# A recurrence chain among projections: updates by heads, halves of the copies swapped, and an ordering clock with other lags

## The chip, the core and the metric

The kernel runs on one core of a Trainium2 chip. The core's engines work side by side, each through its own queue in order: TensorE (PE in the profile, its weight loads PEld), VectorE (DVE), ScalarE (ACT), GpSimd (POOL) and SyncE (SP), which here starts transfers. They meet only at semaphores. The metric is the time of one launch in microseconds (us) on the device; several runs are taken, and their median counts.

## The reference

One inference step of a decoder layer in float32, for a prompt of 1024 positions and for 8 sequences of 4 new positions (the sample), with a width of 1024:

```
z = x @ w_in                       # 62 column tiles of 128 for each part of the input
RWKV-7 branch, 16 heads of 64:     # token shift, then for every position
    sa = S @ (-kk);  S = S * decay + sa (kk * a)^T + v k^T;  y = S @ r
    group norm, bonus, gate
RG-LRU branch:                     # convolution of 4, two block gates, a linear recurrence, gelu gate
mix = (gate_a * yA + gate_b * yB) @ w_o;  h1 = LN(alpha * x + mix)
y = LN(alpha * h1 + (silu(h1 @ w_gate) * (h1 @ w_up)) @ w_down)
```

Outputs are y for both parts and the new states. The step `S = ...` is a recurrence over 1024 positions; the rest is matmuls and work by element.

## The kernel before

**Projections.** The main line of the program runs matmuls of 128 x 128 weights against up to 512 columns, as three products of split operands (`xh`, `xl`, `wh`, `wl`; ScalarE makes the high parts `wh`, VectorE the low parts `wl`). A tile of w_in is 24 matmuls for each piece of columns, in one of two PSUM banks; a task evacuates it. `STREAM` fixes the order of the tiles: RK, V, XB and GATE groups for units 0 to 7. The first four units are the first half of the positions with the sample, the last four the second half. After w_in come w_o and the FFN, which is projections nearly alone.

**The chain of a unit.** A unit is four heads (two pairs `i`, two heads `h` of 64 rows each: head 0 on partitions 0 to 63, head 1 on 64 to 127) over 512 positions. These are cut into 8 chunks of 64. The task `stage` copies the operands and works out the inverses (`inverse`); then `chain(u)` (L996) runs its 8 chunks, 0 to 7, one after the other, for each:

- `cx` (L1073): four small matmuls of `arm` with the state in `su`; their result is copied from PSUM to `xs`, the rows of head 0 by ScalarE, those of head 1 by VectorE (L1074, L1075).
- `ahead(c + 1)`: two ScalarE operations make `bkh`, TensorE transposes `vz` and `bkh` for the next chunk.
- `cu` (L1085): four matmuls of `nz` with `xs`; their result is copied to `su`, again in two halves (L1086, L1087). `ahead_evac` follows: three ScalarE copies for the next chunk, `bkt` among them.
- `cs` (L1098): four matmuls of `bkt` with `su`; then four VectorE updates (L1103) make the state of the next chunk: state times decay plus `cs`, one for each pair and head, in the order pair 0 head 0, pair 0 head 1, pair 1 head 0, pair 1 head 1.

Each step needs the one before. `outputs` (16 more small matmuls a chunk), `finish`, `sample`, `lru` and the stages of the next unit are further tasks. Unit u + 1 may copy its first operands when u's chain is half done, and its others when it has ended.

**What sets the order.** The program is written out by a `Ticker`: each task is a generator of instructions, the main line is another, and a model (`Clock`) keeps a time for each engine. An instruction of a task is issued when the model thinks that its operands are ready and its engine is free, otherwise the main line goes on; `ready` (L168) adds a lag of 0.2 us to the end of a producer on another engine. The real engines keep the order written out, whatever the true times, and the semaphores between them are put in from the operands. For the two copies of a half into one tile, they make the second wait for the first; the model does not know of that.

## Time and profile before

| | |
|---|---|
| median of 3 runs | 2136.09 us (2135.69 to 2139.7) |
| the profiled execution's own time | 2141.15 us |
| its span, first to last instruction | 2139.4 us |
| mean granted TensorE clock | 0.971 |
| TensorE busy | 2042.7 us, 95% of the span |
| VectorE busy | 1224.1 us, 57% |
| ScalarE busy | 1072.9 us, 50% |
| GpSimd busy | 381.4 us, 18% |

The profile is one execution; times in it are microseconds from the first instruction. Its rows name engine, line, operation, output and inputs, and how many instructions stand in a group. In the profile all matmuls of the main line have the line 255 and nearly everything else 325, because helpers record them; the tiles' names tell them apart. `bank<-xx,wh` is a projection, `bank<-su,arm` is `cx` or an output, `bank<-xs,nz` is `cu`, `bank<-su,bkt` is `cs`. A small matmul of this chain shows as two matmuls in the trace. "<-" behind a wait names what ended it. The granted clock is TensorE's: 1.00 is full, and the trace has 0.5 beside it.

### The profile page before, as it was taken

Reading aid. Unit: us, or ns where it says so; the run is one execution under the profiler, and the core shown is the slowest. Engines: PE = TensorE matmul, PEld = TensorE weight load, DVE = VectorE, ACT = ScalarE, POOL = GpSimd, SP = SyncE. Lnnn points to the kernel's source line nnn. Section 1 sums busy time; section 2 is a strip of 40 time slices with the busy share of each in tenths; the row PEclk is TensorE's granted clock in tenths of the full one; section 3 lists DMA queues with packets and bytes.
Section 4 is the critical chain, followed back from the end, with each engine's and each line's share of the span. In section 5 each row is a group of like instructions: output and inputs, shape, how many; then the busy total and the mean of one; then the engine's idle time right before and its main releaser. Section 6 shows DMA issues by size and latency. Waiting matters only on the chain.

```text
span 2139.4 us, 43960 instructions
## 1 busy us (share of the span) xinstructions
PE 2042.7 (95%) x17664; PEld 1771.1 (83%) x17664; DVE 1224.1 (57%) x2967; ACT 1072.9 (50%) x2476; POOL 381.4 (18%) x797
## 2 busy tenths in 40 slices
PE   7799989999999999898999799999999999999997
PEld 7798988998877777676777697889999998999987
DVE  5586796797785785867868656522222322222226
ACT  4657777766766668576777536821121122112221
POOL 1111211212211310201112010221111211111124
PEclk9899999999999999999999799999999999999999
DMA  4131232231241222222223414211111111111112
GB/s 138 56 103 60 64 84 69 66 103 61 65 132 52 81 83 64 69 66 67 84 73 86 139 66 134 89 66 38 56 50 32 58 42 46 42 51 50 45 45 81
DMA packets 124923, 152.82 MB, mean 71 GB/s; under 512 B 82784, under 2 KB 87296, under 8 KB 124720
## 3 DMA queue, kind: packets, MB, share of 16 engines
q0 software_dynamic: 31936, 112.75, 15.6%
q1 hardware_dynamic: 92784, 37.28, 7.0%
q8 instruction: 138, 2.26, 0.4%
q14 instruction: 65, 0.53, 0.1%
HBM read 132.45 MB, written 17.57 MB: 70 GB/s over the span
## 4 chain that ended last, share of the span: by engine, by line
PE 85%; DVE 6%; ACT 6%; DMA 2%; issue 2%; SPq 0%; POOL 0%; DVEq 0%; ACTq 0%; POOLq 0%
PE bank L255 68%; PE bank L325 17%; DVE tmp L325 1%; ACT bk L325 1%; ACT arm L325 1%; DVE wl L325 1%; ACT wh L325 1%; ACT tmp L325 1%; DVE yb L325 0%; ACT accB L325 0%; DVE su L325 0%; DVE arm L325 0%; ACT su L325 0%; ACT nz L325 0%; DVE btmp L325 0%
## 5 line engine op out<-in xcount | busy, mean ns | idle before, releaser
L255 PE MATMUL bank<-xx,wh 128*128 128x512 f32 (+4 forms) x3168 | 808.7, 341 | 45.0 <-DVE rge L325 14.4
L255 PEld LDWEIGHTS bank<-xx,wh 128*128 128x128 f32 x3168 | 547.4, 194 | 109.0 <-ACT rge L325 15.6
L255 PE MATMUL bank<-xx,wl 128*128 128x512 f32 (+4 forms) x1584 | 534.6, 337 | 0.0
L325 DVE TENSOR_TENSOR wl<-wraw,wh 128x512 fp32r<-128x512 f32 (+2 forms) x336 | 263.7, 786 | 272.1 <-ACT wh L325 270.1
L325 ACT ACTIVATE wh<-wraw 128x512 fp32r<-128x512 f32 (+2 forms) x408 | 245.3, 609 | 267.1 <-PE bank L255 242.1
L255 PE MATMUL bank<-hl,wh 128*128 128x272 f32 (+1 forms) x1056 | 342.3, 324 | 0.2 <-DVE hl L325 0.2
L255 PE MATMUL bank<-hh,wh 128*128 128x272 f32 (+1 forms) x1056 | 341.3, 323 | 1.0 <-ACT hh L325 1.0
L255 PE MATMUL bank<-hh,wl 128*128 128x272 f32 (+1 forms) x1056 | 341.5, 323 | 0.0
L255 PEld LDWEIGHTS bank<-xx,wl 128*128 128x128 f32 x1584 | 306.2, 193 | 28.0 <-issue 3.1
L255 PEld LDWEIGHTS bank<-hh,wh 128*128 128x128 f32 x1056 | 198.7, 188 | 17.3 <-ACT hh L325 1.2
L255 PEld LDWEIGHTS bank<-hl,wh 128*128 128x128 f32 x1056 | 198.7, 188 | 16.2 <-DVE hl L325 0.5
L255 PEld LDWEIGHTS bank<-hh,wl 128*128 128x128 f32 x1056 | 198.6, 188 | 15.3
L325 POOL DMA_DIRECT2D wraw<-in_win x114 | 61.8, 542 | 724.4 <-DVE wl L325 469.0
L325 POOL TENSOR_TENSOR wl<-wraw,wh 128x512 fp32r<-128x512 f32 (+1 forms) x72 | 86.4, 1200 | 512.0 <-ACT wh L325 489.7
L255 PE MATMUL bank<-u,wh 128*128 128x272 f32 (+1 forms) x768 | 176.7, 324 | 0.0
L255 PEld LDWEIGHTS bank<-u,wh 128*128 128x128 f32 x768 | 128.6, 188 | 11.3
L325 DVE TENSOR_TENSOR acc<-acc,bank 128x272 f32<-128x272 f32 (+3 forms) x96 | 49.9, 519 | 148.0 <-PE bank L255 148.0
L325 ACT ACTIVATE sg<-bank 128x272 f32<-128x272 f32 (+1 forms) x66 | 30.8, 466 | 196.1 <-PE bank L255 196.1
L255 PE MATMUL bank<-u,wl 128*128 128x272 f32 (+1 forms) x384 | 124.3, 324 | 0.0
L325 DVE TENSOR_TENSOR sg<-sg,bank 128x272 f32<-128x272 f32 (+1 forms) x66 | 34.3, 520 | 155.7 <-PE bank L255 155.7
L325 ACT ACTIVATE su<-bank 64x256 f32<-64x256 f32 (+1 forms) x192 | 59.9, 338 | 63.3 <-PE bank L325 59.0
L325 ACT ACTIVATE u<-sg 128x272 fp32r<-128x272 f32 (+1 forms) x66 | 33.0, 501 | 111.8 <-DVE sg L325 111.8
(248 smaller groups left out, 3162.9 us busy)
## 6 DMA issues: line engine op xcount, KB each, us to landing
wraw<-in_win POOLq DMA_DIRECT2D x116, 512.0 KB, 3.6
wraw<-in_wgu POOLq DMA_DIRECT2D x48, 512.0 KB, 3.5
wraw<-in_wo POOLq DMA_DIRECT2D x16, 512.0 KB, 3.6
wraw<-in_wdn POOLq DMA_DIRECT2D x16, 384.0 KB, 3.4
wraw<-in_wdn POOLq DMA_DIRECT2D x16, 320.0 KB, 3.1
mgd<-yb POOLq DMA_DIRECT2D x32, 128.0 KB, 2.5
out_y<-tmp SPq DMA_DIRECT2D x8, 512.0 KB
scrN<-nz SPq DMA_DIRECT2D x64, 32.0 KB
```

What stands on the lines that cost most here:

```text
L255: fn(*args, **kw)
L325: fn(*args, **kw)
```

## The change

Three edits. The updates of the state go by heads: both pairs of head 0, then both of head 1. Of the two copies behind `cx` and of the two behind `cu`, the lower half (head 0) goes to VectorE and the upper (head 1) to ScalarE, and VectorE's is issued first. The ordering clock's lag depends on the engine of the producer: 0.2 us for TensorE and DMA as before, 0.137 for ScalarE, 0.127 for VectorE, 0.06 for GpSimd.

```diff
+    LAG = {"PE": 0.2, "ACT": 0.137, "DVE": 0.127, "POOL": 0.06, "DMA": 0.2}
...
-                        lag = 0.2
+                        lag = self.LAG[e2]
...
-                A(xs[0:64, :, 0], cx[0:64])
-                TC(xs[64:128, :, 1], cx[64:128])
+                TC(xs[0:64, :, 0], cx[0:64])
+                A(xs[64:128, :, 1], cx[64:128])
...
-                A(su[0:64, :, 1, 0], cu[0:64])
-                TC(su[64:128, :, 1, 1], cu[64:128])
+                TC(su[0:64, :, 1, 0], cu[0:64])
+                A(su[64:128, :, 1, 1], cu[64:128])
...
-                for i in range(2):
-                    for h in range(2):
+                for h in range(2):
+                    for i in range(2):
                         hb = slice(64 * h, 64 * h + 64)
                         to = sn[hb, i, 0, h] if c < 7 else sst[hb, 2 * pr + i]
                         STT(to, su[hb, i, 0, h], pc[hb, i, c:c + 1], cs_[hb, i], OP.mult, OP.add)
```

`A` is a ScalarE copy, `TC` a VectorE copy, `STT` a VectorE update. One line is added, so lines behind it have numbers one higher. Since the order of the whole program is made by the clock, instructions move on every engine, from about the first unit to the end of w_o.

**The two copies**, in unit 1, chunk 5. VectorE before; `bank_71` holds `cx` and `cu`, and "waits" names the engines whose semaphores an instruction waits for:

```order
L325 COPY xs<-bank_71 64x2x64 [waits Activation_49]
L325 SCALAR_TENSOR_TENSOR tmp<-kta_198,dv,tmp 128x548 [waits DMAHW6_49,DMAHW4_49,DMAHW7_49,DMAHW3_49,DMAHW0_49]
L325 TENSOR_TENSOR tmp<-tmp,bank_68 128x512 [waits DMAHW1_49,PE_49]
L325 TENSOR_TENSOR tmp<-tmp,pcs_137 128x512 [waits DVE_49]
L325 COPY su_150<-bank_71 64x2x64 [waits Activation_49]
```

VectorE now:

```order
L326 TENSOR_TENSOR tmp<-tmp_94,cst 128x512 [waits Activation_49]
L326 COPY xs<-bank_71 64x2x64 [waits PE_49]
L326 TENSOR_TENSOR tmp<-tmp,bank_67 128x512 [waits DMAHW3_49,PE_49,Activation_49]
L326 TENSOR_TENSOR tmp<-tmp,pcs_137 128x512 [waits DVE_49]
L326 COPY su_150<-bank_71 64x2x64 [waits PE_49,Activation_49]
```

ScalarE before:

```order
L325 ACTIVATE xs<-bank_71 64x2x64 [waits DVE_49,PE_49]
L325 ACTIVATE bkh<-bk,pc_135 128x128 x2
L325 ACTIVATE su_150<-bank_71 64x2x64 [waits DVE_49,PE_49]
L325 ACTIVATE su_151<-bank_70 64x4x64
L325 ACTIVATE su_152<-bank_70 64x4x64
L325 ACTIVATE bkt_155<-bank_70 128x256
```

ScalarE now:

```order
L326 ACTIVATE xs<-bank_71 64x2x64 [waits DVE_49]
L326 ACTIVATE bkh<-bk,pc_135 128x128 x2
L326 ACTIVATE tmp_94<-bank_69 128x64
L326 ACTIVATE su_150<-bank_71 64x2x64 [waits DVE_49]
L326 ACTIVATE su_151<-bank_70 64x4x64
L326 ACTIVATE su_152<-bank_70 64x4x64
L326 ACTIVATE bkt_155<-bank_70 128x256
```

VectorE's copies waited for ScalarE and now wait for TensorE (and, for `su`, an earlier ScalarE operation); ScalarE's waited for TensorE and now wait for VectorE. What stands behind them on ScalarE (`bkh`, `su`, `bkt`) is the same.

**TensorE in the chain of unit 1** (`bank_71` as above, `bank_70` for transposes; `xx` rows are the projection). Before, from chunk 5's `cx` on:

```order
L325 MATMUL bank_71<-su_150,arm 64x64 [waits DVE_49]
L325 MATMUL bank_71<-su_150,arm 64x64 x3
L255 MATMUL bank_66<-xx,wl_79 128x256
L255 MATMUL bank_66<-xx,wh_77 128x256
L325 MATMUL bank_68<-tmp 64x512 [waits DVE_49]
L325 MATMUL bank_68<-tmp 64x512
L255 MATMUL bank_66<-xx,wh_77 128x256
L255 MATMUL bank_66<-xx,wl_79 128x256
L255 MATMUL bank_66<-xx,wh_77 128x256 x2
L255 MATMUL bank_66<-xx,wl_79 128x256
L255 MATMUL bank_66<-xx,wh_77 128x256 x2
L255 MATMUL bank_66<-xx,wl_79 128x256
```

Now, from chunk 6's `cx` to its `cs`:

```order
L326 MATMUL bank_71<-su_151,arm 64x64 [waits DVE_49]
L326 MATMUL bank_71<-su_151,arm 64x64
L326 MATMUL bank_71<-su_151,arm 64x64 [waits Activation_49]
L326 MATMUL bank_71<-su_151,arm 64x64
L326 MATMUL bank_67<-tmp 128x256 [waits Activation_49]
L326 MATMUL bank_70<-cst,vz_126 64x128 x2
L326 MATMUL bank_70<-cst,bkh 128x128 [waits Activation_49] x2
L326 MATMUL bank_71<-xs,nz 64x64 [waits DVE_49]
L326 MATMUL bank_71<-xs,nz 64x64 x3
L326 MATMUL bank_68<-tmp_96,cst 128x292
L326 MATMUL bank_71<-su_151,bkt_155 64x64 [waits Activation_49]
L326 MATMUL bank_71<-su_151,bkt_155 64x64 x3
```

The small matmuls of the chain follow each other without a row of the projection. The same holds for all 91 rows from the transposes in chunk 3 to the end of this unit's chain; the projection goes on behind them with its second tile of XB2.

**TensorE at the start of the last unit's chain**, where w_in has ended and w_o begins (`128x272` rows are w_o). Before, from chunk 2's `cs` to chunk 3's `cu`:

```order
L325 MATMUL bank_71<-su_151,bkt_155 64x64 [waits DVE_49]
L325 MATMUL bank_71<-su_151,bkt_155 64x64 x3
L325 MATMUL bank_71<-su_152,arm 64x64 [waits DVE_49]
L325 MATMUL bank_71<-su_152,arm 64x64
L325 MATMUL bank_71<-su_152,arm 64x64 [waits Activation_49]
L325 MATMUL bank_71<-su_152,arm 64x64
L325 MATMUL bank_70<-cst,vz_126 128x128 [waits Activation_49]
L325 MATMUL bank_70<-cst,vz_126 128x128
L325 MATMUL bank_70<-cst,bkh 128x128 [waits Activation_49] x2
L325 MATMUL bank_71<-xs,nz 64x64 [waits DVE_49]
```

Now, around chunk 2's `cx`:

```order
L256 MATMUL bank_66<-xx,wh_77 128x272 x2
L256 MATMUL bank_66<-xx,wl_79 128x272
L256 MATMUL bank_66<-xx,wh_77 128x272 x2
L256 MATMUL bank_66<-xx,wl_79 128x272
L326 MATMUL bank_71<-su_151,arm 64x64 [waits DVE_49]
L326 MATMUL bank_71<-su_151,arm 64x64 x3
L256 MATMUL bank_66<-xx,wh_77 128x272 x2
L256 MATMUL bank_66<-xx,wl_79 128x272
L256 MATMUL bank_66<-xx,wh_77 128x272 x2
L256 MATMUL bank_66<-xx,wl_79 128x272
L256 MATMUL bank_66<-xx,wh_77 128x272 x2
L256 MATMUL bank_66<-xx,wl_79 128x272
```

Before, the next chunk's `cx` and `cu` follow with no row of w_o between. Now 9 matmuls of w_o (6 of them shown) stand between chunk 1's `cs` and this `cx`, and 12 (9 shown) between it and chunk 2's `cu`.

## The prediction

> **What bounds the kernel now.** I read the page first, then the busy time by stretches, then who waits for whom, and last the timeline of single chunks of the chain. Of the page, the span, TensorE's busy time, the clock by fortieths of the span, and the shares of the chain that ended last:
>
> ```profile
> span 2139.4 us, 43960 instructions
> ...
> PE 2042.7 (95%) x17664; PEld 1771.1 (83%) x17664; DVE 1224.1 (57%) x2967; ACT 1072.9 (50%) x2476; POOL 381.4 (18%) x797
> ...
> PEclk9899999999999999999999799999999999999999
> ...
> PE 85%; DVE 6%; ACT 6%; DMA 2%; issue 2%; SPq 0%; POOL 0%; DVEq 0%; ACTq 0%; POOLq 0%
> ```
>
> TensorE is busy for 2042.7 of 2139.4 us, and it makes up 85% of the chain that ended last. So the change can only win back what TensorE loses: 96.7 us of idle time, and the slices in which the clock row shows less than 9. The other engines matter where they make TensorE wait. Four stretches of the same kernel (us from the span's start; busy time of PE, PEld, DVE, ACT, POOL; then granted clock, DMA share, GB/s):
>
> ```profile
> 324.00:392.00 68.00, 67.83 (x872) 58.24 (x873) 48.09 (x121) 46.09 (x127) 10.40 (x31) 1.00 0.20 66
> 862.00:882.00 20.00, 16.14 (x124) 10.26 (x123) 16.29 (x41) 8.95 (x22) 5.18 (x16) 0.91 0.24 67
> 1182.00:1231.00 49.00, 37.85 (x515) 29.85 (x515) 33.43 (x87) 31.28 (x76) 4.01 (x15) 0.72 0.49 141
> 1400.00:1450.00 50.00, 50.00 (x317) 45.61 (x317) 13.86 (x19) 11.69 (x23) 8.89 (x10) 1.00 0.14 48
> ```
>
> The last row, in the FFN, shows what TensorE does without any chain: 50.00 of 50 us at clock 1.00, so nothing can be won there. The first row is the whole chain of unit 1 in the kernel before: 67.83 of 68 us at clock 1.00. A chain whose steps lie between projection matmuls costs almost nothing. The second and third rows are places where the chain runs nearly bare, with few or no projection matmuls between its steps. 862 to 882 us has 3.9 us idle, and a clock of 0.91 that takes another 0.09 x 20 = 1.8 us: 5.7 of 20 us, 28%. 1182 to 1231 us, the first chunks of the last unit, has 11.2 us idle and 0.28 x 49 = 13.7 us of clock: 24.9 of 49 us, 51%. (Clock loss counts whole stretches, so it is an upper bound where TensorE also idles.) This third stretch is the largest loss in the middle of the kernel.
>
> What TensorE waited for between 100 and 1300 us (total, times, longest); the first two rows are a projection that waits until its banks are evacuated, the others are the chain:
>
> ```profile
> PE bank L255 <- DVE rge L325: 11.5, 4, 5.6
> PE bank L255 <- ACT rge L325: 7.3, 2, 3.9
> PE bank L325 <- DVE su L325: 5.5, 10, 1.3
> ...
> PE bank L325 <- ACT bkh L325: 4.4, 4, 2.3
> ...
> PE bank L325 <- ACT su L325: 3.6, 2, 2.6
> ...
> PE bank L325 <- ACT bkt L325: 0.4, 1, 0.4
> PE bank L325 <- DVE xs L325: 0.3, 1, 0.3
> ```
>
> The chain's rows sum to 5.5 + 4.4 + 3.6 + 0.4 + 0.3 = 14.2 us. That is all that TensorE directly loses to the chain's hops; the rest of the loss in bare stretches is clock, and waits for other things.
>
> **The change part by part.** Every matmul, copy and update is still there, none added. Three things move. One chunk of the chain, late in the last unit (start, us, engine, operation):
>
> ```profile
> 1245.33 1.21 DVE L325 SCALAR_TENSOR_TENSOR su<-su,pc,bank 64x64 f32<-64x64 f32 x4
> ...
> 1248.28 0.27 ACT L325 ACTIVATE xs<-bank 64x128 f32<-64x128 f32 x1 [5.07 <-PE bank L325]
> ...
> 1248.45 0.69 ACT L325 ACTIVATE bkh<-bk,pc 128x128 f32<-128x128 f32 x2
> ...
> 1248.58 0.29 DVE L325 COPY xs<-bank 64x128 f32<-64x128 f32 x1 [0.85 <-ACT xs L325]
> ...
> 1250.30 0.38 PE L325 MATMUL bank<-cst,bkh 128*128 128x128 f32 x2
> ...
> 1250.62 0.46 PE L325 MATMUL bank<-xs,nz 128*64 128x64 f32 x8
> ...
> 1251.13 0.54 ACT L325 ACTIVATE su<-bank 64x128 f32<-64x128 f32 x2 [2.00 <-PE bank L325]
> ...
> 1251.43 0.30 DVE L325 COPY su<-bank 64x128 f32<-64x128 f32 x1 [2.56 <-ACT su L325]
> ...
> 1253.45 0.46 PE L325 MATMUL bank<-su,bkt 128*64 128x64 f32 x8
> ```
>
> *The four state updates by heads.* The first row: four updates of 64 partitions in 1.21 us, 0.30 apart. Before, they alternate between the lower and the upper 64 partitions; now the two lower ones come first, then the two upper ones. No row of before shows two such updates on the same partitions, so I bound the gain. None: still 0.30 apart. Most: from two operations on the same partitions, by the next rows, where the second starts 0.10 us after the first, which took 0.18:
>
> ```profile
> 482.11 0.18 DVE L325 TENSOR_TENSOR rge<-rge,pp 128x32 f32<-128x32 f32 x1
> ...
> 482.21 0.72 DVE L325 SCALAR_TENSOR_TENSOR tmp<-tmp,tmp 128x548 f32<-128x548 f32 x1
> ```
>
> There the follower starts 0.08 us before the other ends; in the updates it starts 0.02 after. A saving of 0.10 us at two of the four places is 0.2 us a chunk, 64 x 0.2 = 13 us of VectorE time in all, and I take that value. On TensorE it is worth little: VectorE is not the bound (the waits for su are 5.5 us in all), and in covered chunks the projection's matmuls hide it. I take 0, with 0 to -3 us as ends.
>
> *Lower halves on VectorE, upper on ScalarE.* The rows at 1248.28 and 1248.58 show that the two copies don't run side by side: VectorE's starts 0.30 us after ScalarE's, which took 0.27. The views of waits and the order (VectorE's copy waits for an ScalarE semaphore) agree:
>
> ```profile
> DVE su L325 <- ACT su L325: 58.7, 41, 5.7
> ...
> DVE xs L325 <- ACT xs L325: 34.7, 34, 4.5
> ```
>
> Now VectorE's copy comes first and ScalarE's waits for it. Whether a hand-over costs more in one direction than in the other is seen where both happen in the FFN:
>
> ```profile
> 1415.11 0.44 DVE L325 TENSOR_TENSOR sg<-sg,bank 128x272 f32<-128x272 f32 x1 [1.17 <-PE bank L255]
> ...
> 1415.59 0.43 ACT L325 ACTIVATE u<-sg 128x272 fp32r<-128x272 f32 x1 [1.85 <-DVE sg L325]
> ...
> 1416.05 0.44 DVE L325 TENSOR_TENSOR u<-sg,u 128x272 fp32r<-128x272 f32 x1 [0.50 <-ACT u L325]
> ```
>
> VectorE to ScalarE: 1415.11 + 0.44 to 1415.59, 0.04 us. ScalarE to VectorE: 1415.59 + 0.43 to 1416.05, 0.03 us. So the pair takes the same, and the next matmul has both halves at the same time as before. What is late next is ScalarE's queue: behind its copy of xs stand the two bkh operations (1248.45), which TensorE transposes before it may take the next step, and behind its copy of su stand the three copies that prepare the next chunk. They now start 0.30 us later, and later still when VectorE is in a long operation; VectorE in turn no longer stands still for ScalarE (58.7 + 34.7 us). In the chunk shown the bkh operations end at 1249.14 and their transposes start at 1250.30, 1.2 us later, so 0.3 us is hidden there. If the cover is gone, it is 2 x 0.3 us a chunk.
>
> *Shorter lags.* The clock that sets the order now believes that a result of ScalarE, VectorE or GpSimd is ready 0.06 to 0.14 us earlier. The rows just read (0.03 and 0.04 us after the recorded end) say that this is nearer the truth. So steps of the chain stand earlier in TensorE's order. Counted in the order: between the cu matmuls and the cs matmuls of a chunk stand 398 projection matmuls before and 238 now over the 64 chunks, and 26 of the 64 hops have none, against 15. From the end of the cu matmuls (1250.62 + 0.46) to the end of VectorE's copy (1251.43 + 0.30) it takes 0.65 us, so a hop without cover stalls by about that. I take 11 more such hops at a half of 0.65, as other units' small matmuls stand in some: +3 us, with 0 and 11 x 0.65 = +7 as ends.
>
> *The order itself.* This is the largest part. It changes nearly everywhere between 100 and 1300 us, and three places decide.
>
> (a) The last unit's first chunks, 1182 to 1231 us. TensorE's rows there, in the order of before:
>
> ```profile
> 1192.83 0.70 PE L325 MATMUL bank<-xs,nz 128*64 128x64 f32 x8
> 1194.24 0.70 PE L325 MATMUL bank<-su,bkt 128*64 128x64 f32 x8 [0.71 <-DVE su L325]
> 1196.61 0.59 PE L255 MATMUL bank<-xx,wh 128*128 128x272 f32 x1 [1.67 <-ACT xx L325]
> 1198.01 0.70 PE L325 MATMUL bank<-su,arm 128*64 128x64 f32 x8 [0.80 <-DVE su L325]
> ...
> 1205.16 0.46 PE L325 MATMUL bank<-su,arm 128*64 128x64 f32 x8 [0.35 <-DVE su L325]
> ...
> 1210.43 0.46 PE L325 MATMUL bank<-su,arm 128*64 128x64 f32 x8 [1.33 <-DVE su L325]
> ...
> 1218.43 1.05 PE L325 MATMUL bank<-zt,p 32*32 32x16 f32 x64 [2.30 <-DMA zt<-scrZ]
> ```
>
> Stalls on the chain (0.71, 0.80, 0.35, 1.33 us), on the split of the merged input (1.67) and on a transfer (2.30). Counted in the order, ahead of the second, third and fourth chunk stood 1, 3 and 0 projection matmuls; now 1, 9 and 15. If the stretch ran like 324 to 392 us, 24.9 us would be saved; if the splits and the transfers hold the projection itself, nothing. The stalls 1.67 and 2.30 and their like stay, say 5 us with as much clock; so I take -15 us, with 0 and -25 as ends.
>
> (b) Unit 1, chunks 3 to 7 (counted from 0). In the new order the projection stops before the second tile of XB2, where main_xb waits for a free scratch tile, and 150 small matmuls of chain, sample and the next unit follow without one of the projection: four chunks bare. A bare chunk takes 5.3 to 7.2 us by the rows at 1198.01, 1205.16 and 1210.43, so the stretch is 21 to 29 us, where the old order lost nothing (first row of the stretches). It is as rich in other small matmuls as 862 to 882 us, so I take that stretch's 28%: 25 x 0.28 = +7 us; ends 0 (the small matmuls fill it) and 25 x 0.51 = +13. [...]
>
> (c) 862 to 882 us. The bare run there is shorter in the new order (10 of its rows wait, before 14): a third of 5.7, -2 us; ends 0 and -6. (d) The borders of units, where a projection waits for its evacuation: 11.5 + 7.3 us in six waits before. The new order has such rows as well, at RK3 for one, with eight small matmuls ahead of it; whether they sum to more or less can't be read from an order, so I take 0, with -9 and +9 as ends.
>
> Sum: 0 + 3 - 15 + 7 - 2 + 0 = **-7 us**. The profiled execution took 2141.15 us (span 2139.4), so it would be 2134; the median of the runs shown is 2136.09, 5.06 below the profiled one, so the forecast is **2129 us**.
>
> **The rivals.** *The loss only moves* (chance 0.25). TensorE's work is the same, and a bare stretch saved at the end was bought with one in unit 1. For it: the sum of extra waits in bare runs is about the same in both orders. With (a) at -12, (b) at +10 and +3 for the hops, it is +1 - 2 = -1 us: 2135. *Slower* (0.27). The mechanism is the stretch (b): if its clock falls as from 1182 to 1231 us it costs 13 us, the hops cost 7, and (a) saves no more than 5 because the splits of the merged input, not the chain, hold TensorE there (the stall of 1.67 us on ACT xx speaks for it; the four stalls on su speak against it): +15 us, 2151. It decides as soon as (a) saves less than (b) and the hops cost. *More than that* (0.1): (a) at its end of -25, (b) at 3, hops at 0, (c) -3: -25 us, 2111. That the halves simply undo what the updates and lags gain is part of the first rival: 0.3 us a hop against 0.2 us and the lags.
>
> **How the numbers follow.** Forecast 0.38, the rivals 0.25, 0.27 and 0.10. The likeliest one's own range, with half its bounds, is 2121 to 2136. Since cases of both signs hold much, the 8-in-10 range reaches from the best case to the slow one: 2110 to 2152. A measurement of this kernel tells 0.2%, 4.3 us, from no change: faster than 2131.8 are most of the forecast (0.31), the best case (0.10) and some of the first rival (0.06): 0.47. Slower than 2140.4: the slow case but for its near end (0.25), and 0.03 of the first two: 0.28. Between: 0.25.
>
> **What the profile after would show.** The four updates in about 1.0 us instead of 1.21. ScalarE's copies of xs and su waiting for VectorE, and no wait of VectorE for ScalarE's. A stretch near 300 to 400 us, about 25 us long, with TensorE busy below 90% and a clock below 1.00 where it was 67.83 of 68 at 1.00. At the end of the last unit a clock above 0.85 and the waits for su gone. If the clock stays at 1.00 in unit 1, (b) is wrong; if the stretch before the output projection is as slow as before, (a) is wrong and with it the sign. Waits for rge well over the 18.8 us of before would be (d), which I left at 0.

## The result, and the profile after

The kernel with the change takes 2174.21 us (median of four runs, 2170.95 to 2177.53), against 2137.89 us for the kernel before measured beside it: a ratio of 1.0155, with a 95% interval of 1.0138 to 1.0173. It is **33 to 36 us slower** (by the ratio and by the medians). The prediction was 2129 us, with 2110 to 2152 as its range: wrong in sign and in size. The profiled execution took 2171.7 us. From its page, the span, the busy times and the clock by fortieths of the span:

```profile
span 2169.7 us, 43984 instructions
...
PE 2068.6 (95%) x17664; PEld 1786.7 (82%) x17664; DVE 1207.1 (56%) x2967; ACT 1092.2 (50%) x2477; POOL 374.4 (17%) x797
...
PEclk9899999899989999899999799999999999999999
```

TensorE has the same 17664 matmuls and is busy for 26 us longer, and the clock row has five slices below 9, where before it had two. Its idle time grew by only 4.4 us, from 96.7 to 101.1. So the profile books the time as longer matmuls more than as waiting. TensorE's waits between 100 and 1300 us (total, times, longest), the larger rows and those that the prediction spoke of:

```profile
PE bank L326 <- ACT tmp L326: 9.3, 10, 2.4
PE bank L326 <- ACT yb L326: 6.3, 2, 5.5
PE bank L326 <- ACT su L326: 5.7, 9, 1.4
PE bank L256 <- DVE rge L326: 5.3, 2, 4.2
PE bank L326 <- DMA zt<-scrZ: 5.1, 1, 5.1
PE bank L326 <- ACT nz L326: 4.0, 1, 4.0
...
PE bank L256 <- ACT rge L326: 2.7, 2, 1.5
...
PE bank L326 <- DVE su L326: 2.3, 2, 2.0
```

All rows of this view sum to 56.8 us, and to 59.1 us before. The waits for rge, which the prediction feared, fell from 18.8 to 8.0 us; others (tmp, yb, nz: tasks of other units) came in their place. **This list does not show a loss of 33 to 36 us at all.**

To find it, I took each TensorE matmul's time to the start of the next, less the usual step of its shape at full clock, and summed: 381.7 us of loss before, 411.5 after, 29.8 more (the profiled executions are 30.5 apart). Of the 29.8, 17.5 lie in times of half clock (waits in those times included), 6.6 in steps from one shape of matmul to another, 3.0 between matmuls of one shape, and only 2.7 in gaps above 0.35 us at full clock. The time at half clock grew from 124.9 to 151.3 us. Projection matmuls of 512 columns follow each other in 0.233 us at full clock and in 0.427 at half clock (medians, before); by that ratio these 26.4 us cost 12 us, an estimate, and the runs with extra matmuls below put their price lower still.

Since the matmuls of the projections come in the same sequence in all orders, the loss can be laid side by side by their number, wherever they lie in time. The last two columns belong to the first two experiments:

```
projection matmul   us before  us after   loss before   more after   old order,    new order,
                                                                     new instr.    old instr.
    0 -  767             9          9        37.9          +1.7          0.0          +0.9
  768 - 1055           154        156        21.8          +6.4         +0.7          +4.0
 1056 - 1631           230        239        32.0          -6.9         +1.3          -7.2
 1632 - 1727           357        353        10.9         +13.0         +0.5          +9.3   (b)
 1728 - 1823           384        398         2.8          -2.7          0.0          -2.7
 1824 - 1919           400        410         5.9          +8.1          0.0          +8.1   RK3
 1920 - 2111           423        437         3.8          +1.4          0.0          +1.4
 2112 - 2303           454        474         9.0         +13.8          0.0         +14.1
 2304 - 2687           498        539        28.1          -9.3         +1.3          -9.3
 2688 - 2879           588        616        15.2         +21.4         -0.5         +21.4
 2880 - 3359           646        700        59.1         -24.2         +1.9         -24.1
 3360 - 3455           847        871        25.9          +4.9         +1.0          +3.0   (c)
 3456 - 4127           902        930        70.0          -3.5         +2.8          -5.4
 4128 - 4223          1167       1191        36.2          -5.6         +1.2          -5.4   (a)
 4224 - end           1230       1247        23.2         +11.4         +0.1         +10.1
```

It is a sum of large terms of both signs. Six of these places in the view of busy times by stretches (us; busy PE, PEld, DVE, ACT, POOL; granted clock, DMA share, GB/s), after:

```profile
352.70:397.90 45.20, 41.27 (x417) 32.42 (x416) 26.99 (x78) 28.62 (x73) 2.69 (x5) 0.89 0.11 34
410.10:436.70 26.60, 18.36 (x130) 17.51 (x129) 14.52 (x42) 16.02 (x46) 11.54 (x47) 0.81 0.23 65
474.40:538.90 64.50, 63.14 (x966) 53.47 (x965) 44.88 (x133) 41.40 (x111) 7.86 (x26) 0.95 0.24 71
616.50:699.80 83.30, 77.41 (x926) 58.81 (x926) 52.49 (x150) 44.59 (x111) 9.48 (x29) 0.86 0.24 70
699.80:871.00 171.20, 170.59 (x1463) 129.98 (x1461) 132.40 (x305) 134.62 (x285) 25.40 (x67) 1.00 0.25 76
1191.50:1247.30 55.80, 44.17 (x617) 34.60 (x615) 40.77 (x103) 32.16 (x71) 4.41 (x12) 0.76 0.55 156
```

and the same projection matmuls before:

```profile
357.30:384.30 27.00, 26.83 (x277) 22.78 (x276) 22.43 (x55) 15.32 (x46) 5.42 (x16) 1.00 0.18 61
399.90:422.60 22.70, 22.28 (x170) 20.31 (x169) 14.48 (x35) 18.27 (x47) 8.11 (x27) 1.00 0.20 70
453.80:498.30 44.50, 44.50 (x763) 40.34 (x761) 36.20 (x97) 32.81 (x80) 3.22 (x6) 1.00 0.35 96
587.80:645.60 57.80, 53.75 (x635) 42.74 (x634) 48.28 (x141) 34.35 (x81) 6.04 (x15) 0.97 0.43 135
645.60:847.40 201.80, 192.69 (x1756) 145.57 (x1755) 140.09 (x330) 138.67 (x312) 32.40 (x81) 0.94 0.23 69
1166.60:1229.70 63.10, 51.12 (x746) 39.99 (x745) 46.48 (x114) 38.55 (x90) 6.89 (x25) 0.78 0.49 142
```

The first rows are (b), the first bare stretch: 41.27 of 45.2 us busy at a clock of 0.89, where before TensorE was busy nearly throughout at 1.00. The second is the border at RK3; at the third and fourth, between 474 and 700 us, the prediction did not look: clock 1.00 and 0.97 before, 0.95 and 0.86 now. The fifth is what the new order won: 9.1 us of idle time shrank to 0.6, and the clock rose from 0.94 to 1.00. The last is (a), and it is hardly better than before, though for another reason. Until 1206.2 us TensorE is busy throughout at 1.00; the two parts behind that, ahead of the chain's first copy and from it on, are:

```profile
1206.20:1226.70 20.50, 10.51 (x246) 7.70 (x245) 17.23 (x50) 13.48 (x30) 0.59 (x2) 0.55 0.81 243
1226.70:1247.30 20.60, 18.96 (x310) 15.73 (x309) 9.06 (x24) 11.09 (x29) 0.00 (x0) 0.78 0.42 113
```

The second row, the chain's first chunks, has TensorE busy for 18.96 of 20.6 us, with no wait for su. The first row is new: the small matmuls of the last unit's first inverses stand bare between the end of w_in and the chain, and TensorE is busy for 10.51 of 20.5 us at a clock of 0.55. The wait of 5.1 us for the transfer into zt in the list above lies here. Before, these inverses ran between matmuls of w_in, from 1173 to 1183 us.

### The profile page after: what moved, and what is told of

It is laid out like the page before. It is cut to its first block, busy times and chain, and to the rows that moved or that the text cites. A ratio compares the mean times of both kernels' runs of the same rounds, so it can differ in the third digit from the quotient of the medians.

```text
span 2169.7 us, 43984 instructions
## 1 busy us (share of the span) xinstructions
PE 2068.6 (95%) x17664; PEld 1786.7 (82%) x17664; DVE 1207.1 (56%) x2967; ACT 1092.2 (50%) x2477; POOL 374.4 (17%) x797
## 4 chain that ended last, share of the span: by engine, by line
PE 63%; DVE 5%; ACT 4%; issue 1%; DMA 1%; SPq 0%; DVEq 0%; ACTq 0%
PE bank L256 53%; PE bank L326 10%; DVE tmp L326 1%; DVE wl L326 1%; ACT tmp L326 1%; ACT wh L326 1%; DVE yb L326 0%; ACT L326 0%; ACT su L326 0%; ACT nz L326 0%; DVE bt L326 0%; DVE su L326 0%; DVE btmp L326 0%; ACT bkh L326 0%; ACT bk L326 0%
## 5 line engine op out<-in xcount | busy, mean ns | idle before, releaser
L256 PEld LDWEIGHTS bank<-xx,wl 128*128 128x128 f32 x1584 | 307.7, 194 | 27.3 <-issue 2.9
L256 PEld LDWEIGHTS bank<-hh,wh 128*128 128x128 f32 x1056 | 199.0, 188 | 19.4 <-ACT hh L326 3.0
L256 PEld LDWEIGHTS bank<-u,wh 128*128 128x128 f32 x768 | 128.5, 188 | 11.4
L326 ACT ACTIVATE su<-bank 64x256 f32<-64x256 f32 (+1 forms) x192 | 65.8, 342 | 73.0 <-DVE su L326 59.3
```

Of the source, the lines that this page charges most:

```text
L256: fn(*args, **kw)
L326: fn(*args, **kw)
```

## The experiments

**The order and the instructions apart.** The ordering model can be shown one operation while another is written out in its place; `AS` takes both, the planned one and the one that is issued. So the edited copies and updates were put into the places of the old ones, with TensorE's order that of before row by row, and the other way round. For xs (su and the updates likewise):

```diff
-                A(xs[0:64, :, 0], cx[0:64])
-                TC(xs[64:128, :, 1], cx[64:128])
+                AS("ACT", "activation", (xs[0:64, :, 0], cx[0:64], AF.Copy), dict(bias=0.0, scale=1.0),
+                   lambda: raw.vector.tensor_copy(xs[0:64, :, 0], cx[0:64]))
+                AS("DVE", "tensor_copy", (xs[64:128, :, 1], cx[64:128]), {},
+                   lambda: raw.scalar.activation(xs[64:128, :, 1], cx[64:128], AF.Copy, bias=0.0, scale=1.0))
```

> The new instructions (updates by heads, lower halves on VectorE, upper on ScalarE) in the order of before: the model still plans the old instructions with a lag of 0.2, and the new ones are put into their places, so TensorE's order is that of before, row by row. Theory A (the loss is the order: which small matmuls stand without a projection matmul between them): within 5 us of before, 2133 to 2143, with the clock stretches of before. Theory B (the copies: ScalarE's half now waits for VectorE's, and bkh and bkt behind it come 0.3 us later): at least half of the loss stays, 2152 or more.

> The old instructions (updates pair by pair, lower halves on ScalarE, upper on VectorE) in the order of after: the model plans the new instructions with the new lags, the old ones are put into their places. Theory A: as slow as after, 2168 to 2182 (the updates are 0.2 us longer a chunk). Theory B: at least half of the loss is gone, 2157 or less.

Measured: the new instructions in the old order 2152.67 us, ratio 1.0063 (1.0046 to 1.0079); the old instructions in the new order 2159.61 us, ratio 1.0099 (1.0074 to 1.0124). Neither theory has it alone (the first run just reaches the 2152 of theory B, with a third of the loss, not half). Multiplied, 1.0063 x 1.0099 = 1.0163, the two account for the whole (1.0155). So about 13 us are the instructions and about 21 us the order. The instructions cost about as much in the new order, where 1.0155 / 1.0099 = 1.0055 is 12 us. The table's last two columns show the difference in kind: the instructions cost 0 to 3 us in many places, the order gives and takes up to 24 us at single ones.

**Lags and edits as causes of the order.** The table of lags alone in the kernel before; and the change without it (`lag = 0.2`).

> Only the table of lags, so the instructions are those of before in a third order. Theory C (the lags are too short, so the chain's matmuls stand too early and TensorE waits for hops): 2155 to 2175, most of the loss. Theory A says only that the order decides and not in which direction: anywhere from 2120 to 2180, with as many microseconds as its clock stretches and bare runs give.

> The copies and updates of after, planned with the old lag of 0.2 us for all engines. Theory C: near before, 2130 to 2148. Theory B: as slow as after, 2165 to 2180. Theory A: a fourth order, anywhere from 2120 to 2180; if lags alone and this one do not add up to the loss of 36 us, the edits have no prices of their own.

Measured: the lags alone 2163.27 us, ratio 1.0113 (1.0091 to 1.0135); the change without them 2182.68 us, ratio 1.0198 (1.0183 to 1.0213), slower than with them. By theory C the second should have been near before. The two losses, 24 and 42 us, sum to 66 us, not to 33 or 36: the edits have no prices that add up.

**Copies or updates.** Each alone in the old order; then the new engines with ScalarE's copy issued first again; then both edits with bkh moved ahead of cx on ScalarE.

> Only the copies swapped (lower half on VectorE and first, upper on ScalarE), updates as before, in the order of before. In the run with both edits in the order of before bkh ended 1.37 us (median) after the first copy of xs began, against 0.86 before, and it was 13 us slower. Theory D (the swap puts ScalarE's copy, and so bkh, half a microsecond later): all of the 13 us and the 2 us that the updates save, 2150 to 2156 against 2138 to 2142 for before. Theory E (something else in the pair of edits): under 2146.

> Only the updates by heads, copies as before, in the order of before. Theory D: 0 to -4 us against before, since four updates take 0.18 us less and the next chunk's cx starts so much earlier where no projection matmul covers it. Theory E: slower than before by 5 us or more.

> The copies on the engines of after (lower on VectorE, upper on ScalarE), but ScalarE's is issued first, so that VectorE's waits for it as before; updates as before; order of before. Theory D: the loss is in who goes first, not in which half: within 4 us of before. If the half counted (ScalarE on partitions 64 to 127, VectorE on 0 to 63): as slow as with the swapped copies alone, 2150 or more.

> Both edits in the order of before, and ScalarE's two bkh operations moved from behind its copy of xs to ahead of cx, in all chunks but those where their input is not there yet (chunks 3 and 7 have none to move). Theory D: bkh no longer hangs on the copy of xs, so at least half of the 13 us comes back, 2146 or less, unless the copy of su behind it costs as much. Theory E: no change against both edits without it, 2150 to 2156.

Measured: the copies alone 2156.23 us, 1.0076 (1.0058 to 1.0093); the updates alone 2142.71 us, 1.0006 (0.9995 to 1.0018); ScalarE first 2143.52 us, 1.0016 (1.0003 to 1.0029); bkh ahead 2152.28 us, 1.0054 (1.0040 to 1.0067). So **the instructions' cost is in the copies, and nearly all of it in who goes first, not in which half**: on the swapped halves, with ScalarE first, 16 us shrink to 3 (1 to 6 by the interval). The updates are worth nothing that can be measured. The run with bkh ahead lies in the range of theory E: moving bkh gave at most a little back.

What the late ScalarE copy delays shows in TensorE's waits with the copies alone swapped, where the row for bkh is 9.2 us in eight waits, against 4.4 in four before (the second row is cu waiting for ScalarE's copy of xs):

```profile
PE bank L325 <- ACT bkh L325: 9.2, 8, 3.5
...
PE bank L325 <- ACT xs L1082: 0.6, 1, 0.6
```

Over the 64 chunks, bkh ended 0.86 us (median) after the first copy of xs began, and 1.37 us with the copies swapped: 0.5 us later, not 0.3. Counted from the end of cx it is 0.96 and 1.97 us, 1.0 us later, because the first copy begins later as well. One chunk of the kernel after (start, us, engine, operation):

```profile
1231.61 0.46 PE L326 MATMUL bank<-su,arm 128*64 128x64 f32 x8
...
1231.65 0.73 DVE L326 SCALAR_TENSOR_TENSOR xx<-rge,xx 128x544 fp32r<-128x544 f32 x1
1232.41 0.28 DVE L326 COPY xs<-bank 64x128 f32<-64x128 f32 x1
...
1232.78 0.27 ACT L326 ACTIVATE xs<-bank 64x128 f32<-64x128 f32 x1 [1.55 <-DVE xs L326]
...
1233.09 0.69 ACT L326 ACTIVATE bkh<-bk,pc 128x128 f32<-128x128 f32 x2
...
1233.55 0.77 PE L326 MATMUL bank<-cst,bkh 128*128 128x128 f32 x2
...
1234.25 0.70 PE L326 MATMUL bank<-xs,nz 128*64 128x64 f32 x8
```

cx ends at 1232.07, but VectorE is still in an earlier operation until 1232.38; then comes its copy, 0.09 us after its end ScalarE's, and only behind that bkh, which ends at 1233.78. The transposes, for which only bkh was missing, follow it, and cu starts at 1234.25, 1.2 us after the copies. The run with bkh ahead of cx was to free the transposes. It did, and most of the loss stayed, because another wait took the place:

```profile
PE bank L325 <- ACT xs L1095: 3.1, 3, 2.2
...
PE bank L325 <- ACT bkh L325: 2.3, 4, 0.6
...
PE bank L325 <- ACT bkh L1087: 1.5, 2, 0.9
```

The first row is again cu waiting for ScalarE's copy of xs, now 3.1 us, since 0.7 us of bkh lie in front of that copy. The sum is 6.9 us, where both edits without the move have 8.8 for bkh and 0.4 for xs.

**bkh on GpSimd**, ahead of cx, so that ScalarE has neither in its way (against the run with bkh ahead):

```diff
-   raw.scalar.activation(bkh[:, j], bk[:, j, c + 1], AF.Copy, bias=0.0, scale=pc[:, j, c + 1:c + 2])
+   raw.gpsimd.tensor_scalar(bkh[:, j], bk[:, j, c + 1], pc[:, j, c + 1:c + 2], None, op0=OP.mult)
```

> Both edits in the order of before, with the two bkh operations (not those of chunks 0 and 4) taken off ScalarE and given to GpSimd, issued ahead of cx. Ahead of cx on ScalarE they had freed the transposes (no more waits for bkh) but put 0.7 us in front of the copy of xs, and the 13 us stayed. Theory D2 (the 13 us are ScalarE's queue in the chain: its copy now comes second, and what it has to do before and behind it counts): most of it comes back, 2137 to 2146 against 2138 to 2142 for before. If it stays at 2150 or more, ScalarE's queue in the chain isn't the cause (or GpSimd's own operations and the weight loads behind them in its queue cost as much).

Measured: 2151.25 us, ratio 1.0043 (1.0028 to 1.0058). About a third came back, within the intervals perhaps nothing; at 2150 or more, its expectation says, ScalarE's queue in the chain isn't the cause, or GpSimd's own work costs as much. TensorE's waits:

```profile
PE bank L325 <- ACT xs L1095: 4.1, 3, 2.8
...
PE bank L325 <- ACT bkh L325: 2.5, 5, 0.6
...
PE bank L325 <- POOL bkh L1087: 2.2, 4, 1.5
```

The first transposes now start on time (0.1 us earlier in sum than before), so GpSimd's work does not hold them, and cu waits for ScalarE's copy of xs instead (4.1 us, longest 2.8). The traces show why that copy is late: it waits for VectorE's, and VectorE often can't begin when cx ends. With ScalarE first, ScalarE was still in an earlier operation, by 0.1 us or more, in 21 of the 64 chunks, 19.0 us in sum; with the copies swapped, VectorE was in 42, 39.6 us in sum. Sums over the 64 chunks in the order of before, in us, from each run's trace:

```
                        end of cx to     end of cu to     end of cx to    end of cu to
                        both halves      both halves      start of cu     start of cs
                        of xs copied     of su copied
before                       73.6             57.3            172.8           137.3
ScalarE first                73.0             58.3            175.6           140.2
copies alone                 87.3             71.1            183.1           142.8
both edits                   82.6             68.8            180.2           141.3
both, bkh ahead              89.9             62.4            178.5           140.7
both, bkh on GpSimd          81.0             59.6            181.1           140.7
```

TensorE's order is the same in all six, so the last two columns hold the same matmuls, and what they grow by is lost time. With the copies alone they grow by 10.3 and 5.5 us, 15.8 of the 16.2 us between the two profiled executions: **the loss lies in the two hops behind the copies**. Two delays are in it, the late bkh and the late start of the pair on VectorE. With bkh off ScalarE 8.3 and 3.4 us stay. No run takes the late start alone away, so that it carries the rest is read from the traces, not shown by a run. Matched matmul by matmul with the trace of before, the steps that lead to the transposes of bkh are 5.9 us longer in sum with both edits (7.5 with the copies alone).

**Is before's order a good draw?** Three changes of the model that have nothing to do with the edit, and one in the direction of the lags, a sixth of their size; the instructions are those of before in all four:

```diff
-    FIXED = {"PE": 0.003, "ACT": 0.093, "DVE": 0.07, "POOL": 0.13, "SP": 0.0}
+    FIXED = {"PE": 0.003, "ACT": 0.093, "DVE": 0.0701, "POOL": 0.13, "SP": 0.0}     # first run
+    FIXED = {"PE": 0.003, "ACT": 0.094, "DVE": 0.07, "POOL": 0.13, "SP": 0.0}       # second
+    FIXED = {"PE": 0.003, "ACT": 0.093, "DVE": 0.07, "POOL": 0.131, "SP": 0.0}      # third
...
-                        lag = 0.2
+                        lag = 0.19                                                  # fourth
```

> The kernel before, with one number of the model changed that has nothing to do with the edits: the fixed cost of a VectorE operation is 0.0701 us instead of 0.07. All instructions are the same; the plan is made anew and differs from about the first unit on. Theory A2 (the order of before is one of the better ones among many that the model may make, and any new plan loses about what the order of after lost): 2150 to 2175 against 2138 to 2142 for before. Theory F (the lags and the swapped operations that the model sees make the plan worse): 2132 to 2147, on either side of before.

> As the run before, with the fixed cost of a ScalarE operation at 0.094 us instead of 0.093. Theory A2: 2150 to 2175. Theory F: 2132 to 2147.

> The kernel before with the model's fixed cost of a GpSimd operation at 0.131 us instead of 0.13, the third change of the model that has nothing to do with the edits; it gave +5 us for VectorE's and +27 for ScalarE's. Theory A2 (the order of before is a good draw): slower than before by 4 to 35 us. Theory F: within 6 us on either side.

> The kernel before with a lag of 0.19 us instead of 0.2 for all engines, a small step in the direction of the edit. Theory A2: slower by 4 to 35 us, as any other plan. Theory C (shorter lags are bad by themselves, in proportion): a sixth of what the lags alone cost (24 us), about +4 us or less, so 2138 to 2147.

Measured: 1.0021 (1.0010 to 1.0032), 1.0122 (1.0095 to 1.0149), 0.9988 (0.9974 to 1.0002) and 1.0145 (1.0123 to 1.0166); in us +4, +26, -3 and +31. Theory C falls: a lag shorter by 0.01 us costs as much as the whole table of lags (24 us) or more. Theory F falls with the second run, where 1 ns more for ScalarE in the model costs as much as the order of the change. Theory A2 as written, that any new order is slower by as much, falls with the first and third. What remains: **a new order costs anything from about 0 to 31 us, whatever made it**. Of the seven new orders in these runs (these four, the lags alone, the order of after, and the change without lags less its copies' 13 us, an estimate) none is measurably faster than before, and five cost 21 to 31 us. That before's order lies at the good end is what the seven show; why it does, they don't.

**What the clock is worth in a bare stretch.** Extra matmuls that nobody reads, put ahead of TensorE instructions that had waited, keep it busy meanwhile. The table FILLERS has the number of the waiting TensorE instruction and how many:

```diff
+    def warm(self, e):
+        if e == "PE":
+            n = self.FILLERS.get(self.npe, 0)
+            self.npe += 1
+            if n:
+                self.filler(n)
...
+        def filler(n):
+            to = (Bk.free or G.free)[:1]              # a PSUM bank that is free
+            x = cst.bitcast(mybir.dt.bfloat16)
+            for _ in range(n if to else 0):
+                nc.tensor.matmul(to[0][:, 0:256], x[:, 0:128], x[:, 0:256], start=True, stop=True)
```

> The kernel before in its order, with extra matmuls (128x128 bf16 weights, 256 columns, into a PSUM bank that is free at that place, read by nobody) ahead of those TensorE instructions that waited 0.35 us or longer in the trace between 100 and 1320 us: 349 for 38 waits of 56 us in all, three quarters of each wait; 10 of the 38 places have no free bank and get none. In the traces the clock falls for steps of 3.41 us, nearly always after a step in which TensorE was busy below 0.6. Theory G (a bare stretch costs mostly through the clock, and the clock follows TensorE's busy share in the step before): half-clock time falls from 125 us to 60 to 90, and the time by 8 to 25 us, 2115 to 2132. Theory H (the clock doesn't depend on whether TensorE waits, or only on the kind of work): half-clock time stays near 125 us and the time within 4 us of before, or up to 10 us above.

> The same for the kernel after in its order: 370 extra matmuls for 41 waits of 0.35 us or longer in its trace between 100 and 1420 us. Theory G: 10 to 25 us below after, 2150 to 2164, and half-clock time from 151 us to 80 to 115. Theory H: 2168 to 2184.

Measured: on before 2153.73 us, ratio 1.0053 (1.0033 to 1.0074), half-clock time 103.9 instead of 124.9 us; on after 2167.56 us, 1.0119 (1.0099 to 1.0140) where after alone is 1.0155, half-clock time 96.7 instead of 151.3 us. So the clock does follow TensorE's busy share, as theory G says, though on before the half-clock time stayed above its range of 60 to 90 us. But both times miss G's ranges, and half-clock time turned out to be worth little: on after 55 us less of it gave 7 to 8 us, and the two intervals just meet. On before, fillers that waited for their bank to be evacuated spoiled it; L637 is the filler:

```profile
PE bank L637 <- ACT tmp L340: 7.4, 3, 4.1
PE bank L637 <- DVE tmp L340: 4.3, 1, 4.3
PE bank L637 <- DVE rb L340: 3.8, 1, 3.8
PE bank L637 <- ACT rge L340: 3.6, 1, 3.6
```

Where they did not wait they show what the clock is worth, less what the fillers take themselves. The last unit's first chunks, the stretch that has 0.78 in the last row of before above, with fillers:

```profile
1180.60:1239.50 58.90, 52.23 (x813) 39.74 (x812) 46.57 (x113) 38.41 (x90) 5.49 (x17) 0.97 0.53 152
```

Clock 0.97 instead of 0.78, 27.3 us at half clock down to 3.4 (counted in the traces), and the stretch takes 58.9 instead of 63.1 us. **4 us, not the 13.7 that the prediction counted.** The rest of the 36 us lost there stayed with the clock at 0.97, so it is not the clock's.

> The kernel before with extra matmuls only where they did not wait for their PSUM bank in the first run with fillers (147 ahead of 21 waits), and 67 more ahead of three waits between 71 and 89 us. Where they had waited (0.7 to 4.3 us each at seven places) they cost about 20 us; in the last unit's first chunks they took the half-clock time from 27 to 3 us and saved 4 us. If that adds up place by place: 4 to 10 us below before, 2130 to 2138. If fillers cost elsewhere what they save there: within 3 us of before.

Measured: 2138.07 us, ratio 0.9985 (0.9974 to 0.9997), and the same stretch:

```profile
1169.00:1228.70 59.70, 52.44 (x814) 39.49 (x814) 46.63 (x114) 38.67 (x90) 5.99 (x20) 0.97 0.53 150
```

59.7 us, 3.4 less than before. Outside the places with fillers the two traces agree to 0.7 us per 96 projection matmuls. At one place (from projection matmul 2784 on) the fillers lost 3 us; the clock fell at 609.2 us there, and at 613.6 before.

**A kernel faster than both?** The third new order, with the updates by heads in place, and then with fillers only where at least two of the three small banks are free.

> The updates by heads (copies and lags as before) in the order that the model makes with 0.131 us for GpSimd, which was 0.12% below before (interval 0.9974 to 1.0002). If the updates by heads are worth what they save on VectorE where nothing covers it (0.18 us a chunk; -3.2 us between two profiles, +1.3 between the medians, in the order of before): 0 to 4 us below that order, 2134 to 2141 against 2142 for before. If that order's small gain was noise: 2138 to 2144.

> The same with extra matmuls ahead of those waits of 0.35 us or longer in that order's trace at which at least two of the three banks for small products are free (so that a filler hardly waits). The fillers chosen in the order of before gave 3 us: another 0 to 5 us below the run without fillers, 2131 to 2139. If the clock in bare stretches is worth less than the fillers' own time: no gain or up to 4 us above.

Measured: without fillers 2141.69 us, ratio 1.0000 (0.9987 to 1.0013): the small gain of that order was noise, and the updates gave none. With fillers 2135.32 us, ratio **0.9963 (0.9948 to 0.9978)**, 7 to 8 us below before and some 40 below after. Its page:

```profile
span 2132.1 us, 44283 instructions
...
PE 2045.7 (96%) x17831; PEld 1769.9 (83%) x17831; DVE 1215.0 (57%) x2967; ACT 1073.0 (50%) x2475; POOL 385.8 (18%) x797
...
PEclk9899999999999999999999999999999999999999
```

Half-clock time is 86.5 us, against 137.9 in the trace without fillers: 51 us less of it for 6 to 8 us, much the same price as above. The clock row has no slice below 9 after the second.

## Why the prediction was wrong

*The updates by heads: right.* 0 was forecast with 0 to -3 us as ends, and the run with them alone shows no difference. On VectorE they save about what was taken. The groups of the updates and of the copies of xs (count, busy us, mean ns, idle before them and what ended it), after:

```profile
L326 DVE SCALAR_TENSOR_TENSOR su<-su,pc,bank 64x64 f32<-64x64 f32 x224 | 54.0, 278 | 51.5 <-PE bank L326 48.8 <-ACT arm L326 0.7 <-ACT tmp L326 0.2
...
L326 DVE COPY xs<-bank 64x128 f32<-64x128 f32 x64 | 18.0, 281 | 24.1 <-PE bank L326 22.9
...
L326 ACT ACTIVATE xs<-bank 64x128 f32<-64x128 f32 x64 | 17.4, 272 | 74.7 <-DVE xs L326 66.2 <-DVE gs L326 6.3 <-DVE tmp L326 1.6
```

and before:

```profile
L325 DVE SCALAR_TENSOR_TENSOR su<-su,pc,bank 64x64 f32<-64x64 f32 x224 | 62.6, 280 | 28.6 <-PE bank L325 24.2
...
L325 DVE COPY xs<-bank 64x128 f32<-64x128 f32 x64 | 18.9, 295 | 35.9 <-ACT xs L325 34.7
...
L325 ACT ACTIVATE xs<-bank 64x128 f32<-64x128 f32 x64 | 17.0, 266 | 60.9 <-PE bank L325 50.3 <-DVE gs L325 2.9 <-DVE bze L325 2.5
```

224 updates keep VectorE busy for 54.0 instead of 62.6 us, and four in a row take 0.99 instead of 1.21 us (medians). Between two on the same half the next starts 0.20 us after, between halves 0.28 to 0.30, about the length of an update (0.278 us in the row above); before, where each is on the other half than the last, it was 0.29 to 0.30 at all three places (medians).

*The copies: the step "So the pair takes the same, and the next matmul has both halves at the same time as before" was wrong, and so was "0.3 us is hidden there".* The rows in the FFN did not carry over: in the pair of xs the hand-over takes 0.09 us from VectorE to ScalarE and 0.03 the other way (medians), and the pair 0.65 instead of 0.60 us. What counts more is that the pair begins when the engine that goes first is free, and VectorE often wasn't. In the order of before, with the copies alone, both halves were ready 0.21 us later on average behind cx and 0.22 behind cu. ScalarE's idle time that ends with VectorE's copy of xs is now 66.2 us, where VectorE's that ended with ScalarE's was 34.7. And bkh came 1.0 us later after cx, not 0.3; I judged its cover by one chunk that had 1.2 us of it. The median cover over the chunks was 1.1 us before and 0.5 with the copies alone; where it ran out, TensorE waited for bkh, 9.2 us in eight waits instead of 4.4 in four. The copies have no term in the sum, so they were put at nothing, and measured +13 us (+16 alone).

*The lags: +3 us with 0 to +7.* No run can give them a price: the table alone cost 24 us and a lag shorter by 0.01 us cost 31. The count of uncovered hops (26 against 15) is a property of one order, not of a lag.

*(a) -15 us: measured -5.6* (-5.4 with the old instructions). Two steps failed. The first is what was counted: the projection matmuls between the chunks, and not what stands between w_in's end and the first chunk. The chunks did become covered, as forecast: no wait for su is left in them. But the first inverses now stand bare ahead of them, and of the 27.3 us at half clock in this stretch 20.5 begin there, at 1208.3 us. The chain's first cx started 2.7 us after the end of w_in's last matmul before, and 19.4 us after it now. So most of the loss moved ahead of the chain instead of going. The second step is the price: 13.7 of the 24.9 us were the clock times the whole stretch, which the prediction called an upper bound and then spent in good part. With the clock nearly restored the stretch gains 3.4 to 4.1 us. The clock in it after is 0.76, not above 0.85.

*(b) +7 us: measured +13.0* (+9.3 with the old instructions), at the place and with the signs named. The bare run alone, with TensorE busy for 86% of 28.6 us at a clock of 0.85:

```profile
362.50:391.10 28.60, 24.67 (x284) 17.52 (x282) 11.82 (x38) 18.17 (x51) 0.54 (x1) 0.85 0.04 12
```

The mechanism held; the price was at the upper end. Counted as in the prediction, idle time and clock make 3.9 + 4.3 = 8.2 us here; what the other 5 are is not settled.

*(c) -2 us: measured +4.9 (+3.0). (d) 0: at RK3 +8.1.* Between 410.1 and 436.7 us the projection waits 4.2 us for rge, and the eight small matmuls ahead of it wait 4.0 us for tmp; before, the waits there were 0.4 us. The place had been named and priced at 0. Over the whole kernel the waits for rge fell by 10.8 us.

*What is missing.* (a), (b), (c) and RK3 sum to +20.4 of the 29.8 us. Of the rest, +13.8, +21.4 and -24.2 us lie in units 2 to 4, and +11.4 behind (a), where the prediction assigned nothing. Its choice of places was one-sided: it took the worst stretch of before, which had most to gain, and but for (b) left out the stretches at clock 1.00, which could only become worse. With terms of up to 24 us at many places, the sum could lie anywhere in some 30 us, and, as the other new orders showed, mostly above zero.

The rival "slower" (0.27, 2151 us) had the sign, and its sizes for (b), 13 us, and (a), 5 saved, are those measured. But it had the splits of the merged input hold TensorE in (a); the waits for them are 1.9 us there now, and those for zt, of the inverses, 8.0. That the sizes agree is in part luck. It falls short by the copies' 13 us, the border at RK3 and the units in between.

## What to carry to other kernels

When a model writes the order, an edit has two prices, that of its instructions and that of a new order, and the second cannot be derived from the edit: freeze the order to measure the first, and make a few meaningless changes to the model to see the spread of the second. Here the order at hand lay at the good end of that spread, so five of seven new ones lost 21 us or more. In a serial pair of copies, the one who goes first should be the engine that is free when the matmuls end, and behind whose copy stands work that the next matmuls wait for; here that was ScalarE (2143.52 us with its copy first, 2156.23 with VectorE's, on the same halves). A stretch that is given cover may only pass its loss on, so count from the last covered matmul to the first of the chain as well. And in a stretch that waited on other engines, the lower clock was worth far less than its share of the time: 3.4 to 4.1 us, where that share was 13.7.

## What the runs showed of the hardware

In the clock records of before and after, the 34 half-clock times begin on a grid of 3.41 us and last a multiple of it (but for the last of each, which the end of the trace cuts). At full clock, each of the 19 steps of this grid in which TensorE was busy for less than 0.48 was followed by a step at half clock; of the 35 busy for 0.48 to 0.76, 12 were; of those busy for more, only three (0.91, 0.92 and 0.95), which held 54 to 123 mostly small matmuls. In 32 cases the clock came back from half to full, each time after a step busy for 0.92 or more. Of the 34 falls, 27 followed a step busy for less than 0.6. A step in which TensorE was busy for half the time could be enough: 31 of the falls came after a step whose longest gap was 2.8 us or less, four of them below 0.5 us.

In the runs with fillers, the extra matmuls of 128x128 by 256 columns follow each other in 0.109 us at full clock and 0.213 at half clock, so a wait of 1 us takes nine of them. Projection matmuls of 256 columns take 0.118 and 0.213 us to the next (medians, after).

What was not tried: two tiles for the two copies, so that neither waits for the other.
